# A hybrid SSD, gated and latent attention trunk: root of the first norm from logarithm and exponential, gates moved into the last scan step

## The chip, the cores and the metric

The kernel runs on one core of a Trainium2 chip. The metric is device time in microseconds (us), the median of the runs shown. Five engines work side by side, each through its own queue in order: TensorE (PE, matmuls; PEld are its weight loads), VectorE (DVE), ScalarE (ACT), GpSimd (POOL), and SyncE (SP), which here issues most of the transfers.

## The reference, cut to what matters

A trunk of two layers over 512 tokens of width 1024, in float32. The change lies in the first layer, of which this is the part that matters:

```python
h = rms_norm(x, mix_norm_even[j])              # x * rsqrt(mean(x*x) + 1e-6) * w
proj = h @ w_in
z, xbc, dt_raw, q, k, v, g, gk_low = jnp.split(proj, _offsets(IN_SIZES), axis=-1)
# scan mixer: 16 heads in 2 groups, chunks of 128 tokens
dt = jax.nn.softplus(dt_raw + dt_bias)
a_cum = jnp.cumsum(dt * -jnp.exp(a_log), axis=2)
y_ssd = rms_norm_per_group(scan(silu(conv(xbc)), dt, a_cum) * silu(z))
# gated mixer: 4 heads
gk = jax.nn.log_sigmoid(gk_low @ gk_w2 + gk_b) / 16
gcum = jnp.cumsum(gk.reshape(bsz, nc, Q, H, DK), axis=2)   # chunks of 64 tokens
q_dec = q * exp(gcum);  k_inv = k * exp(-gcum)
x = x + jnp.concatenate([y_ssd, y_gla], axis=-1) @ w_out
```

A dense SwiGLU layer, latent attention with 16 heads and a second dense layer follow; the change doesn't touch them.

## The kernel before

Everything is held transposed, 128 features on the partitions and 512 tokens in the row. Each dense product is exact to float32 by parts: every operand is split into a rounded half (`hi`) and a rest (`lo`), and `mm3` (L149) adds three products. `dense` (L154) runs it over 8 blocks of 128 features, so one output tile costs 24 matmuls. A weight tile of 512 KB goes through three steps (L130 to L147): a transfer into one of two raw buffers (`wraw`), a cast on ACT into one of three `whi` buffers, and a subtraction on DVE into one of three `wlo` buffers. Three PSUM banks (`acc`) take the dense products; a bank comes free when its product has been read. Four more banks serve small work: `st` and `a1` one each, `a2` two.

The order of the instructions on each engine is written by a planner before the run. It takes them in program order by readiness under its own cost estimates; `tc.high_priority(offset=n)` moves a block ahead by n instructions, and weights are moved ahead by 90 (`AHEAD`). Buffers are given out in that planned order too. The tiles of a pool that opens after another one closed wait until the closed pool's last reader of that memory is done.

First norm. The eight tiles of x are split (L207 to L214). The norm's factor R is not needed for the dense products, only where their results are read. ACT squares each tile into one of two `sq` buffers, DVE adds them up one after another (L218 to L231), and `rstd` (L173 to L197) sums over partitions with two matmuls into `st` and takes the root on DVE: ten instructions in a row, from a bit trick and two refinement steps. `tok_scalar` (L237) turns R into one number for each token. Behind it stand the product for the step widths and the gates' low rank, `dg` (L292), and the steps: softplus by a series of small instructions on DVE (L307 to L326), a cumulative sum by matmul (L334), and its copies (L336 to L343).

Scan mixer. Eight steps f, two heads each. `conv(i)` (L351) is a dense product, read with R into `xpad` (L358), a four tap convolution and a silu; `z_gate` (L390) a dense product and a silu; `core` (L396) the scan of the two heads, whose tile `mt` has two buffers (L407). After every fourth step `group_norm` (L460) normalises the four tiles of its group (`rstd`, then L464) and splits them into the parts `mxh` and `mxl` (L126, L127), which `out_round` (L267) multiplies by the output weights. In step 7 stand `out_round(0)` and `values(2)` ahead of `core(7)`. `values(h)` (L470) makes the values of one gated head: two weight tiles and 96 matmuls of 256 columns. `values(3)` stands behind `core(7)` and `group_norm(1)` (L505).

Gated mixer. Its pool `gp` opens when the scan's pool `sp` has closed. First come the gates: weights (L513 to L522), four products (L527), their absolute values and minima (L528, L529), Exp (L530), Ln (L531), a subtraction (L532) and four running sums on DVE (L534). `inner(h)` (L542) then makes q (read into `qd`, L558) and k, calls `out_round(1)` for head 0, and goes on to the scores (L594 to L596), the state and the outputs; `outer(h)` multiplies by the output gate.

Of the kernel before, what the change touches and what calls it, by code (L numbers as in the profile page):

```python
# [8 lines left out]
F32 = mybir.dt.float32  # L9
# [9 lines left out]
P = 128  # L19
# [6 lines left out]
AHEAD = 90  # L26
VALUES = (2, 3, 7)
# [19 lines left out]
def kernel(ctx: ExitStack, tc: tile.TileContext, A, yT, stop=99):  # L47
# [11 lines left out]
    def nm(s):  # L59
        cnt[0] += 1  # L60
        return f"{s}_{cnt[0]}"
# [30 lines left out]
    V.memset(warm, 0.0)  # L92
    S.activation(warm, warm, AF.Square)
# [7 lines left out]
    def col(name, i=0, lo=0, hi=P):  # L101
        j = PV[name] + i
        return pv[lo:hi, j:j + 1]
# [16 lines left out]


# [27 lines left out]
    def mm3(out, ah, al, bh, bl, first, last):  # L149
        E.matmul(out, ah, bh, start=first, stop=False)  # L150
        E.matmul(out, ah, bl, start=False, stop=False)  # L151
        E.matmul(out, al, bh, start=False, stop=last)  # L152

    def dense(ps, w, xs):  # L154

        n = len(xs)
        for k, (xh, xl) in enumerate(xs):
            mm3(ps, w[0][:, k, :], w[1][:, k, :], xh, xl, k == 0, k == n - 1)
# [39 lines left out]

    class Norm:
# [18 lines left out]
        def square(self, c, behind=None):  # L218
            x = X[c]
            sq = res.tile([P, T], F32, tag="sq", name=nm("sq"), bufs=2)  # L220
            i = S.activation(sq, x, AF.Square)
            if behind is not None:
                tc.add_manual_dep(i.ins, behind.ins.name,
                                  mybir.DependencyInfo(mybir.DependencyClass.NoSync,
                                                       mybir.DependencyReason.DATA),
                                  reason="squares once all parts are split")
# [35 lines left out]
    for c in range(KD):  # L262
        nrm.square(c, nrm.last)
    R = nrm.done()
# [21 lines left out]
    with tc.tile_pool(name="gkp", bufs=1) as gkp:  # L286
        rtok = tok_scalar(R)
# [15 lines left out]
        nc.sync.dma_start(alog, A["a_log"].partition_broadcast(P))  # L303

        ps = aux()
        for c in range(4):
            E.transpose(ps[:, 16 * c:16 * c + 16], dg[0:16, c * P:(c + 1) * P], ident[0:16, 0:16])  # L307
        dr = gkp.tile([P, 4, 16], F32, name="dr")
        V.tensor_tensor(dr, ps[:, :64].rearrange("p (c h) -> p c h", c=4),
                        dtb.unsqueeze(1).to_broadcast([P, 4, 16]), ALU.add)  # L310
        da = gkp.tile([P, 4, 16], F32, name="da")
        S.activation(da, dr, AF.Abs)
        S.activation(da, da, AF.Exp, scale=-1.0)
        db = gkp.tile([P, 4, 16], F32, name="db")
        V.tensor_scalar(db, da, 2.0, None, ALU.add)
        V.reciprocal(db, db)
        V.tensor_tensor(da, da, db, ALU.mult)
        V.tensor_tensor(db, da, da, ALU.mult)
        dp = gkp.tile([P, 4, 16], F32, name="dp")
        V.tensor_scalar(dp, db, 1.0 / 15, None, ALU.mult)  # L320
        for n in (13, 11, 9, 7, 5, 3):
            V.scalar_tensor_tensor(dp, dp, 1.0 / n, db, ALU.add, ALU.mult)  # L322
        V.scalar_tensor_tensor(dp, dp, 1.0, da, ALU.add, ALU.mult)
        V.tensor_scalar(dr, dr, 0.0, None, ALU.max)
        dt = gkp.tile([P, 4, 16], F32, name="dt")
        V.scalar_tensor_tensor(dt, dp, 2.0, dr, ALU.mult, ALU.add)  # L326
        av = gkp.tile([P, 16], F32, name="av")
        S.activation(av, alog, AF.Exp)
        at = gkp.tile([P, 4, 16], F32, name="at")
        V.scalar_tensor_tensor(at, dt, -1.0, av.unsqueeze(1).to_broadcast([P, 4, 16]),  # L330
                               ALU.mult, ALU.mult)
        ps = aux()
        for c in range(4):
            E.matmul(ps[:16, c * P:(c + 1) * P], at[:, c, :], tri, start=True, stop=True)  # L334
        acf = gkp.tile([16, T], F32, name="acf")
        V.tensor_copy(acf, ps[:16])  # L336
        acd = dpool.tile([16, T], F32, name="acd")
        nc.sync.dma_start(acd, acf)
        ps = aux()
        for c in range(4):  # L340
            E.transpose(ps[:, 16 * c:16 * c + 16], acf[:, c * P:(c + 1) * P], ident[0:16, 0:16])
        act = gkp.tile([P, 4, 16], F32, name="act")
        V.tensor_copy(act, ps[:, :64].rearrange("p (c h) -> p c h", c=4))  # L343


        with tc.tile_pool(name="ssd", bufs=2) as sp:
# [3 lines left out]

            def conv(i, tag, bufs, bank=acc):  # L351
# [3 lines left out]
                dense(ps, w, xp)  # L355
# [127 lines left out]

            rounds = []
            for f in range(8):
# [19 lines left out]
            values(3)  # L505


        with tc.tile_pool(name="gla", bufs=2) as gp:
            rmask = gp.tile([P, T], F32, name="rmask", bufs=1)
            G.memset(rmask, 1.0)  # L510
            G.memset(rmask.rearrange("p (c j) -> p c j", c=8)[:, :, 0:1], 0.0)
            gw = gp.tile([80, T], F32R, name="gw", bufs=1)
            G.memset(gw.bitcast(I32), 0)  # L513
            w2 = res.tile([P, T], F32, tag="sq", name="w2", bufs=2)
            wt = res.tile([P, T], F32R, tag="sq", name="wt", bufs=2)
            for j in (0, 32, 64):
                nc.scalar.dma_start(w2[j:j + 16, :], A["gk_w2"])
            S.copy(wt[0:16, :], w2[0:16, :])
            V.tensor_tensor(gw[0:16, :], w2[0:16, :], wt[0:16, :].bitcast(F32), ALU.subtract)
            for j in (32, 64):  # L520
                S.copy(gw[j:j + 16, :], w2[j:j + 16, :])

            ga = gp.tile([P, 4, T], F32, name="ga", bufs=1)
            gm = gp.tile([P, 4, T], F32, name="gm", bufs=1)
            for h in range(4):
                ps = aux()
                E.matmul(ps, gw[:, h * P:(h + 1) * P], gx, start=True, stop=True)  # L527
                S.activation(ga[:, h, :], ps, AF.Abs, bias=col("gk_b", h))  # L528
                V.tensor_scalar(gm[:, h, :], ps, col("gk_b", h), 0.0, ALU.add, ALU.min)  # L529
            S.activation(ga, ga, AF.Exp, scale=-1.0)  # L530
            S.activation(ga, ga, AF.Ln, bias=1.0)  # L531
            V.tensor_tensor(gm, gm, ga, ALU.subtract)  # L532
            for h in range(4):
                V.tensor_tensor_scan(gm[:, h, :], rmask, gm[:, h, :], 0.0, ALU.mult, ALU.add)  # L534
# [122 lines left out]
            p01 += outer(1, o1)  # L657
            o3 = inner(3)
# [399 lines left out]
```

## Time and profile before

| what | us |
|---|---|
| median of 3 runs | 1372.63 |
| lowest, highest | 1371.01, 1373.25 |
| the profiled execution's own time | 1371.09 |
| its span | 1368.9 |

The span is the time from the first to the last instruction; 2.2 us of the profiled execution's time lie around it. Matmuls overlap: the profile gives one of 512 columns a duration of 0.39 us, but in a full stream one starts every 0.227 us. A row of the timeline gives start, duration, engine, line, operation, output and inputs, shapes, a count, and in brackets the engine's idle time before it and what ended that.

### The profile page before, as it was taken

To read this page: it belongs to the slowest core of one execution; us is meant where nothing else is said; L and a number is where in the kernel's file an instruction comes from. 1 tells how busy PE (TensorE), PEld (TensorE's weight loads), DVE (VectorE), ACT (ScalarE), POOL (GpSimd) and SP (SyncE) were. 2 spreads that over 40 slices of the span, in tenths; PEclk is the share of its full clock that TensorE was granted. 3 is DMA by queue.
4 is the path that set the end of the run, shared out by engine and by line. 5 is a ranking of instruction groups with operands and counts; after the bars stand their busy time and mean duration, and the time that the engine had idled before them with its cause. 6 is when DMAs were issued, how large, how long until landed. Compare 5 with 4: busy or idle time off the path is not lost.

```text
span 1368.9 us, 16667 instructions
## 1 busy us (share of the span) xinstructions
PE 1344.9 (98%) x6506; PEld 1088.7 (80%) x6506; DVE 815.5 (60%) x1369; ACT 562.8 (41%) x941; POOL 7.8 (1%) x35
## 2 busy tenths in 40 slices
PE   8999999999999999999999999999999999999998
PEld 5788889788888888888888887666588888888887
DVE  7987976788867444444333469776594444443221
ACT  5584633544344322332232348775653322322121
POOL 0000000000000000000000000000000000000000
PEclk9999999999999999999999999999999999999999
DMA  5342232222233333223333321111033223323331
GB/s 177 109 141 91 77 95 78 78 77 62 79 93 105 93 94 106 92 92 99 90 100 100 101 68 56 39 47 62 1 98 103 93 93 102 98 93 108 111 103 63
DMA packets 36781, 122.22 MB, mean 89 GB/s; under 512 B 4768, under 2 KB 5792, under 8 KB 36704
## 3 DMA queue, kind: packets, MB, share of 16 engines
q1 hardware_dynamic: 35888, 120.72, 28.1%
q8 instruction: 51, 0.84, 0.2%
q10 hardware_dynamic: 816, 0.46, 0.1%
q14 instruction: 26, 0.21, 0.0%
HBM read 119.03 MB, written 2.13 MB: 89 GB/s over the span
## 4 chain that ended last, share of the span: by engine, by line
PE 90%; DVE 5%; ACT 3%; issue 1%; DMA 1%; SPq 0%; ACTq 0%
PE acc L150 27%; PE acc L151 27%; PE acc L152 27%; PE sco L911 2%; PE ptr L925 1%; PE po L934 1%; DVE wlo L145 1%; PE a L447 1%; PE a L625 0%; PE a L433 0%; PE a L614 0%; PE a L451 0%; ACT whi L144 0%; PE a L627 0%; DVE gm L534 0%
## 5 line engine op out<-in xcount | busy, mean ns | idle before, releaser
L150 PE MATMUL acc<-xh,whi 128*128 128x512 f32 x1144 | 449.1, 393 | 5.2 <-DVE dp L322 2.5
L144 ACT CAST whi<-wraw 128x1024 fp32r<-128x1024 f32 (+2 forms) x221 | 225.8, 1022 | 554.0 <-PE acc L151 436.9
L151 PE MATMUL acc<-xl,whi 128*128 128x512 f32 x1144 | 448.7, 392 | 0.0
L152 PE MATMUL acc<-xh,wlo 128*128 128x512 f32 x1144 | 448.7, 392 | 0.0
L145 DVE TENSOR_TENSOR wlo<-wraw,whi 128x1024 fp32r<-128x1024 f32 (+2 forms) x221 | 261.9, 1185 | 163.2 <-ACT whi L144 163.1
L150 PEld LDWEIGHTS acc<-xh,whi 128*128 128x128 f32 x1144 | 214.9, 188 | 51.2 <-ACT cvt L366 2.8
L152 PEld LDWEIGHTS acc<-xh,wlo 128*128 128x128 f32 x1144 | 215.1, 188 | 44.8 <-DVE wlo L145 0.6
L151 PEld LDWEIGHTS acc<-xl,whi 128*128 128x128 f32 x1144 | 215.1, 188 | 44.5 <-issue 1.4
L152 PE MATMUL acc<-fhh,wlo 128*128 128x512 f32 x288 | 112.0, 389 | 0.0
L150 PE MATMUL acc<-fhh,whi 128*128 128x512 f32 x288 | 112.0, 389 | 0.0
L151 PE MATMUL acc<-fhl,whi 128*128 128x512 f32 x288 | 112.0, 389 | 0.0
L683 DVE TENSOR_TENSOR fu<-acc,R 128x512 f32<-128x512 f32 x44 | 30.4, 691 | 136.2 <-PE acc L152 136.2
L680 DVE TENSOR_TENSOR fg<-acc,R 128x512 f32<-128x512 f32 x44 | 30.4, 691 | 89.0 <-PE acc L152 88.9
L152 PEld LDWEIGHTS acc<-fhh,wlo 128*128 128x128 f32 x288 | 54.1, 188 | 11.3
L151 PEld LDWEIGHTS acc<-fhl,whi 128*128 128x128 f32 x288 | 54.1, 188 | 11.3
L150 PEld LDWEIGHTS acc<-fhh,whi 128*128 128x128 f32 x288 | 54.1, 188 | 11.1
L151 PE MATMUL acc<-mxl,whi 128*128 128x512 f32 x128 | 49.9, 391 | 0.0
L150 PE MATMUL acc<-mxh,whi 128*128 128x512 f32 x128 | 49.8, 391 | 0.0
L152 PE MATMUL acc<-mxh,wlo 128*128 128x512 f32 x128 | 49.7, 390 | 0.0
L911 PE MATMUL sco<-kT,qT 96*128 96x128 f32 (+3 forms) x128 | 42.8, 445 | 1.5 <-DVE mx L914 1.3
L914 DVE CUSTOM_DVE_ANT_0 sc<-sco,am 128x128 f32<-128x128 f32 (+3 forms) x64 | 30.7, 487 | 13.6 <-PE sco L911 11.5
L916 ACT ACTIVATE sc<-sc,mx 128x128 f32<-128x128 f32 (+3 forms) x64 | 35.7, 561 | 7.3 <-DVE mx L914 6.8
(329 smaller groups left out, 1584.8 us busy)
## 6 DMA issues: line engine op xcount, KB each, us to landing
wraw<-in_w_gate_dram SPq DMA_DIRECT2D x44, 512.0 KB, 3.5
wraw<-in_w_up_dram SPq DMA_DIRECT2D x44, 512.0 KB, 3.5
wraw<-in_w_down_dram SPq DMA_DIRECT2D x32, 512.0 KB, 3.6
wraw<-in_w_out_dram SPq DMA_DIRECT2D x16, 512.0 KB, 3.6
wraw<-in_w_xbc_dram SPq DMA_DIRECT2D x12, 512.0 KB, 3.6
wraw<-in_w_down_dram SPq DMA_DIRECT2D x16, 384.0 KB, 3.1
wraw<-in_w_z_dram SPq DMA_DIRECT2D x8, 512.0 KB, 3.5
wraw<-in_w_v_dram SPq DMA_DIRECT2D x8, 512.0 KB, 3.5
```

The source lines that it names most:

```text
L144: S.copy(hi[:, :kc * m], r)
L145: V.tensor_tensor(lo[:, :kc * m], r, hi.bitcast(F32)[:, :kc * m], ALU.subtract)
L150: E.matmul(out, ah, bh, start=first, stop=False)
L151: E.matmul(out, ah, bl, start=False, stop=False)
L152: E.matmul(out, al, bh, start=False, stop=last)
L447: E.matmul(pd[64 * h:64 * h + 64, c * P:(c + 1) * P], xdt[:, c, h, :], mt[:, h, c, :], start=True, stop=True)
L680: V.tensor_tensor(g, pg, R, ALU.mult)
L683: V.tensor_tensor(u, pu, R, ALU.mult)
L911: E.matmul(ps[:, :n], qts[j][:, b * P:(b + 1) * P], kts[j][:, :n], start=True, stop=True)
L914: V.tensor_tensor_reduce(sc[:, :n], ps[:, :n], am[:, T - n:], -scale, 3e38, ALU.add, ALU.min, mx[:, j:j + 1])
L916: S.activation(sc[:, :n], sc[:, :n], AF.Exp, bias=mx[:, j:j + 1], scale=-1.0, accum_out=sm[:, j:j + 1])
L925: E.transpose(ps[:, kb * P:(kb + 1) * P], sc[:, kb * P:(kb + 1) * P], ident)
```

## The change

Four parts.

1. The first norm: its squares go into four buffers of a pool of their own, and `rstd_log` replaces `rstd` there. R is the exponential of minus half the logarithm (both on ACT), followed by one refinement step on DVE. The block is moved ahead by 400. The dummy activation at the start is a Ln instead of a Square.
2. The steps are moved behind the last matmul of the product of `conv(0)` and ahead by 150; `tok_scalar` moves to step 2, where `values(0)` first reads it.
3. The gates move from the start of the gated mixer into step 7, ahead of `out_round(0)`. Their temporaries take buffers of the scan (`cva`, `cvt`, and the two `mt` buffers), Exp and Ln run on halves, and eight running sums of 256 columns replace four of 512. `gm` and `rmask` lie in the outer pool.
4. `values(3)` moves from behind the last scan step to a place behind `outer(1)`, into a buffer of the pool `gp`.

```diff
 AHEAD = 90
+FIRST = 400
+STEPS = 150
 VALUES = (2, 3, 7)
...
-    V.memset(warm, 0.0)
-    S.activation(warm, warm, AF.Square)
+    V.memset(warm, 1.0)
+    S.activation(warm, warm, AF.Ln)
+    eps = const.tile([P, 1], F32, name="eps")
+    V.memset(eps, EPS)
...
+    def order(i, behind, reason):
+
+        tc.add_manual_dep(i.ins, behind.ins.name,
+                          mybir.DependencyInfo(mybir.DependencyClass.NoSync, mybir.DependencyReason.DATA),
+                          reason=reason)
...
-            mm3(ps, w[0][:, k, :], w[1][:, k, :], xh, xl, k == 0, k == n - 1)
+            last = mm3(ps, w[0][:, k, :], w[1][:, k, :], xh, xl, k == 0, k == n - 1)
+        return last
...
+    def rstd_log(ssq, n, pool, tag):
+
+        hi = const.tile([P, T], F32R, tag="rsa", name=nm("rsa"))
+        lo = const.tile([P, T], F32R, tag="rsb", name=nm("rsb"))
+        S.copy(hi, ssq)
+        V.tensor_tensor(lo, ssq, hi.bitcast(F32), ALU.subtract)
+        ps = aux()
+        E.matmul(ps, ones_r, hi, start=True, stop=False)
+        E.matmul(ps, ones_r, lo, start=False, stop=True)
+        R = pool.tile([P, T], F32, tag=tag, name=nm(tag), bufs=1)
+        S.activation(R, ps, AF.Ln, scale=1.0 / n, bias=eps)
+        S.activation(R, R, AF.Exp, scale=-0.5)
+        m, t = ssq, const.tile([P, T], F32, tag="rsa", name=nm("rst"))
+        V.tensor_scalar(m, ps, 1.0 / n, EPS, ALU.mult, ALU.add)
+        V.tensor_tensor(t, R, R, ALU.mult)
+        V.scalar_tensor_tensor(t, m, -0.5, t, ALU.mult, ALU.mult)
+        V.scalar_tensor_tensor(R, t, 1.5, R, ALU.add, ALU.mult)
+        return R
...
-        def square(self, c, behind=None):
+        def square(self, c, behind=None, pool=res, bufs=2):
             x = X[c]
-            sq = res.tile([P, T], F32, tag="sq", name=nm("sq"), bufs=2)
+            sq = pool.tile([P, T], F32, tag="sq", name=nm("sq"), bufs=bufs)
             i = S.activation(sq, x, AF.Square)
             if behind is not None:
-                tc.add_manual_dep(i.ins, behind.ins.name,
...
-    for c in range(KD):
-        nrm.square(c, nrm.last)
-    R = nrm.done()
+    with tc.tile_pool(name="sq0", bufs=4) as sq0:
+        for c in range(KD):
+            nrm.square(c, nrm.last, sq0, 4)
+        with tc.high_priority(offset=FIRST):
+            R = rstd_log(nrm.ssq, D, res, "R")
...
-        rtok = tok_scalar(R)
...
+        def steps(behind):
+
+
+            ps = aux()
+            for c in range(4):
+                i = E.transpose(ps[:, 16 * c:16 * c + 16], dg[0:16, c * P:(c + 1) * P], ident[0:16, 0:16])
+                order(i, behind, "steps behind the product that runs until they are ready")
+            dr = gkp.tile([P, 4, 16], F32, name="dr")
+            V.tensor_tensor(dr, ps[:, :64].rearrange("p (c h) -> p c h", c=4),
...
+            acf = res.tile([P, T], F32, tag="sq", name="acf", bufs=2)[:16]
...
+            return dt, act, acd
...
-                dense(ps, w, xp)
+                mm[i] = dense(ps, w, xp)
...
-            def values(h):
+            def values(h, pool=gkp):
...
-                v = gkp.tile([P, 4, 256], F32, name=f"v{h}")
+                v = pool.tile([P, 4, 256], F32, name=f"v{h}", bufs=1)
...
+            gm = gkp.tile([P, 4, T], F32, name="gm")
+
+            rmask = gkp.tile([P, T // 2], F32, name="rmask")
+            G.memset(rmask, 1.0)
+            G.memset(rmask.rearrange("p (c j) -> p c j", c=4)[:, :, 0:1], 0.0)
+
+            def gates():
+
+                gw = sp.tile([80, T], F32R, tag="cvt", name="gw")
+                G.memset(gw.bitcast(I32), 0)
+                w2 = sp.tile([P, T], F32, tag="cva", name="w2")
+                wt = sp.tile([P, T], F32R, tag="cvt", name="wt")
+                for j in (0, 32, 64):
+                    nc.scalar.dma_start(w2[j:j + 16, :], A["gk_w2"])
+                S.copy(wt[0:16, :], w2[0:16, :])
+                V.tensor_tensor(gw[0:16, :], w2[0:16, :], wt[0:16, :].bitcast(F32), ALU.subtract)
+                for j in (32, 64):
+                    S.copy(gw[j:j + 16, :], w2[j:j + 16, :])
+                gas = [sp.tile([P, 2, T], F32, tag="mt", name=nm("ga")) for _ in range(2)]
+                for h in range(4):
+                    ps = aux()
+                    E.matmul(ps, gw[:, h * P:(h + 1) * P], gx, start=True, stop=True)
+                    S.activation(gas[h // 2][:, h % 2, :], ps, AF.Abs, bias=col("gk_b", h))
+                    V.tensor_scalar(gm[:, h, :], ps, col("gk_b", h), 0.0, ALU.add, ALU.min)
+                for ga in gas:
+                    S.activation(ga, ga, AF.Exp, scale=-1.0)
+                for ga in gas:
+                    S.activation(ga, ga, AF.Ln, bias=1.0)
+                for j, ga in enumerate(gas):
+                    V.tensor_tensor(gm[:, 2 * j:2 * j + 2], gm[:, 2 * j:2 * j + 2], ga, ALU.subtract)
+                for h in range(4):
+                    for t0 in (0, T // 2):
+                        gj = gm[:, h, t0:t0 + T // 2]
+                        V.tensor_tensor_scan(gj, rmask, gj, 0.0, ALU.mult, ALU.add)
...
+                if f == 0:
+                    with tc.high_priority(offset=STEPS):
+                        dt, act, acd = steps(mm[0])
                 zg = z_gate(f)
                 if f == R0F:
+                    gates()
                     out_round(0, rounds[0])
+                if f == VALUES[0]:
+                    rtok = tok_scalar(R)
                 if f in VALUES:
                     values(VALUES.index(f))
...
-            values(3)
...
-            rmask = gp.tile([P, T], F32, name="rmask", bufs=1)
-            G.memset(rmask, 1.0)
-            G.memset(rmask.rearrange("p (c j) -> p c j", c=8)[:, :, 0:1], 0.0)
-            gw = gp.tile([80, T], F32R, name="gw", bufs=1)
-            G.memset(gw.bitcast(I32), 0)
-            w2 = res.tile([P, T], F32, tag="sq", name="w2", bufs=2)
...
             p01 += outer(1, o1)
+            values(3, gp)
             o3 = inner(3)
```

## Rows read from the trace of the kernel before

**Rows 1.** Busy time of two engines over the span, from the page: engine, us and share, count of instructions.

```profile
PE 1344.9 (98%) x6506; PEld 1088.7 (80%) x6506; DVE 815.5 (60%) x1369; ACT 562.8 (41%) x941; POOL 7.8 (1%) x35
```

**Rows 2.** Waits of PE over the whole span: who waited, for whom, us in total, times, longest.

```profile
PE acc L150 <- DVE dp L322: 2.5, 1, 2.5
...
PE a L594 <- DVE ki L575: 1.9, 1, 1.9
...
PE st L181 <- ACT rsa L178: 1.0, 1, 1.0
...
PE a L152 <- DVE wlo L145: 0.5, 1, 0.5
...
PE a L150 <- ACT whi L144: 0.4, 1, 0.4
```

**Rows 3.** Timeline of PE at two of these waits.

```profile
43.33 0.39 PE L151 MATMUL acc<-xl,whi 128*128 128x512 f32 x1
43.56 0.39 PE L152 MATMUL acc<-xh,wlo 128*128 128x512 f32 x1
46.40 0.47 PE L150 MATMUL acc<-xh,whi 128*128 128x512 f32 x1 [2.46 <-DVE dp L322]
...
263.39 0.39 PE L152 MATMUL acc<-xh,wlo 128*128 128x512 f32 x1
265.66 0.27 PE L594 MATMUL a<-qd,ki 128*64 128x64 f32 x1 [1.88 <-DVE ki L575]
```

**Rows 4.** Busy time by stretch: the stretch, then for each engine us and count, then PE's granted clock as a share of 2.4 GHz, DMA share, GB/s.

```profile
44.00:47.00 3.00, 0.60 (x3) 0.54 (x4) 3.00 (x9) 2.08 (x3) 0.10 (x1) 1.00 0.00 0
...
263.00:265.00 2.00, 0.78 (x4) 0.32 (x2) 2.00 (x4) 0.96 (x1) 0.00 (x0) 1.00 0.01 4
...
267.00:269.00 2.00, 2.00 (x7) 1.56 (x6) 2.00 (x4) 0.84 (x3) 0.00 (x0) 0.58 0.00 0
269.00:270.30 1.30, 1.30 (x6) 0.55 (x6) 0.81 (x2) 0.31 (x1) 0.00 (x0) 0.50 0.00 0
```

**Rows 5.** Timeline of ACT and of DVE in the first norm: first squares, the rounded sum of squares, first and last instruction of the root, and the reading of the first `acc` bank.

```profile
10.47 1.14 ACT L221 ACTIVATE sq<-x 128x512 f32<-128x512 f32 x2
...
24.38 0.62 ACT L178 CAST rsa<-sq 128x512 fp32r<-128x512 f32 x1 [0.76 <-DVE sq L230]
...
26.34 0.69 DVE L186 TENSOR_SCALAR sq<-st 128x512 f32<-128x512 f32 x1 [0.61 <-PE st L182]
...
34.44 0.68 DVE L196 SCALAR_TENSOR_TENSOR R<-rst,R 128x512 f32<-128x512 f32 x1
...
45.58 0.68 DVE L358 TENSOR_TENSOR xpad<-acc,R 128x512 f32<-128x512 f32 x1
```

**Rows 6.** Timeline of ACT and DVE in the gates: an activation that reads PSUM, two table loads, an Exp of 512 columns, the subtraction and the running sums.

```profile
250.22 0.69 ACT L528 ACTIVATE ga<-st,pv 128x512 f32<-128x512 f32 x1 [1.87 <-PE st L527]
...
253.81 1.28 ACT L531 ACT_TABLE_LOAD   x1
...
258.55 1.28 ACT L549 ACT_TABLE_LOAD   x1
...
261.24 0.62 ACT L556 ACTIVATE e<-gm 128x512 f32<-128x512 f32 x1
...
257.05 2.29 DVE L532 TENSOR_TENSOR gm<-gm,ga 128x2048 f32<-128x2048 f32 x1 [1.38 <-ACT ga L531]
...
259.86 4.56 DVE L534 TENSOR_TENSOR_SCAN gm<-rmask,gm 128x512 f32<-128x512 f32 x4
```

**Rows 7.** Timeline from the last scan step to the second output round: on PE the first transposes of `core(7)`, the first matmul of q of head 0 and the first of `out_round(1)`; on DVE the splits of the normalised group and the first reading of q; on POOL the first write into the pool `gp`.

```profile
213.15 0.60 PE L422 MATMUL a<-ident,xs 128*128 128x128 f32 x4
...
228.81 0.40 PE L150 MATMUL acc<-xh,whi 128*128 128x512 f32 x1
...
239.71 0.39 PE L150 MATMUL acc<-mxh,whi 128*128 128x512 f32 x1
...
236.04 1.89 DVE L127 TENSOR_TENSOR mxl<-y,mxh 128x512 fp32r<-128x512 f32 x3
...
239.64 0.68 DVE L127 TENSOR_TENSOR mxl<-y,mxh 128x512 fp32r<-128x512 f32 x1
240.36 0.69 DVE L558 SCALAR_TENSOR_TENSOR qd<-acc,R 128x512 f32<-128x512 f32 x1
...
240.52 0.53 POOL L510 MEMSET rmask<- 128x512 f32 x1 [83.59 <-DVE mxl L127]
```

**Rows 8.** Timeline of PE: first and last of the 96 matmuls of `values(2)`.

```profile
201.63 0.28 PE L150 MATMUL acc<-whi,xh 128*128 128x256 f32 x1
...
213.03 0.28 PE L152 MATMUL acc<-whi,xl 128*128 128x256 f32 x1
```

**Rows 9.** Weights and the other engines around the last scan step: DVE's weight rests from 213 to 240.4 us as a group (count, busy us and mean ns, idle time before), a cast on ACT with what it waited for, and busy time by stretch as in rows 4.

```profile
L145 DVE TENSOR_TENSOR wlo<-wraw,whi 128x1024 fp32r<-128x1024 f32 x5 | 6.1, 1221 | 9.1 <-ACT whi L144 9.1
...
234.29 1.05 ACT L144 CAST whi<-wraw 128x1024 fp32r<-128x1024 f32 x1 [0.35 <-PE acc L151]
...
195.00:205.00 10.00, 10.00 (x59) 8.83 (x59) 4.51 (x5) 2.40 (x3) 0.00 (x0) 1.00 0.28 101
205.00:213.00 8.00, 8.00 (x69) 8.00 (x68) 0.01 (x1) 2.18 (x4) 0.00 (x0) 1.00 0.18 61
```

More of the change, by code (lines that the diff above doesn't have):

```diff
@@ L151, in mm3 @@
         E.matmul(out, ah, bl, start=False, stop=False)
-        E.matmul(out, al, bh, start=False, stop=last)
+        return E.matmul(out, al, bh, start=False, stop=last)
     def dense(ps, w, xs):
@@ L216, in add @@
                 self.square(c)
-        def square(self, c, behind=None):
+        def square(self, c, behind=None, pool=res, bufs=2):
             x = X[c]
-            sq = res.tile([P, T], F32, tag="sq", name=nm("sq"), bufs=2)
+            sq = pool.tile([P, T], F32, tag="sq", name=nm("sq"), bufs=bufs)
             i = S.activation(sq, x, AF.Square)
             if behind is not None:
-                tc.add_manual_dep(i.ins, behind.ins.name,
-                                  mybir.DependencyInfo(mybir.DependencyClass.NoSync,
-                                                       mybir.DependencyReason.DATA),
-                                  reason="squares once all parts are split")
+                order(i, behind, "squares once all parts are split")
             if self.ssq is None:
@@ L303 @@
         nc.sync.dma_start(alog, A["a_log"].partition_broadcast(P))
[L305 to L342, printed above, removed]
@@ L343 @@
-        V.tensor_copy(act, ps[:, :64].rearrange("p (c h) -> p c h", c=4))
+        def steps(behind):
[5 more added lines that the diff above has]
+            V.tensor_tensor(dr, ps[:, :64].rearrange("p (c h) -> p c h", c=4),
+                            dtb.unsqueeze(1).to_broadcast([P, 4, 16]), ALU.add)
+            da = gkp.tile([P, 4, 16], F32, name="da")
+            S.activation(da, dr, AF.Abs)
+            S.activation(da, da, AF.Exp, scale=-1.0)
+            db = gkp.tile([P, 4, 16], F32, name="db")
+            V.tensor_scalar(db, da, 2.0, None, ALU.add)
+            V.reciprocal(db, db)
+            V.tensor_tensor(da, da, db, ALU.mult)
+            V.tensor_tensor(db, da, da, ALU.mult)
+            dp = gkp.tile([P, 4, 16], F32, name="dp")
+            V.tensor_scalar(dp, db, 1.0 / 15, None, ALU.mult)
+            for n in (13, 11, 9, 7, 5, 3):
+                V.scalar_tensor_tensor(dp, dp, 1.0 / n, db, ALU.add, ALU.mult)
+            V.scalar_tensor_tensor(dp, dp, 1.0, da, ALU.add, ALU.mult)
+            V.tensor_scalar(dr, dr, 0.0, None, ALU.max)
+            dt = gkp.tile([P, 4, 16], F32, name="dt")
+            V.scalar_tensor_tensor(dt, dp, 2.0, dr, ALU.mult, ALU.add)
+            av = gkp.tile([P, 16], F32, name="av")
+            S.activation(av, alog, AF.Exp)
+            at = gkp.tile([P, 4, 16], F32, name="at")
+            V.scalar_tensor_tensor(at, dt, -1.0, av.unsqueeze(1).to_broadcast([P, 4, 16]),
+                                   ALU.mult, ALU.mult)
+            ps = aux()
+            for c in range(4):
+                E.matmul(ps[:16, c * P:(c + 1) * P], at[:, c, :], tri, start=True, stop=True)
+            acf = res.tile([P, T], F32, tag="sq", name="acf", bufs=2)[:16]
+            V.tensor_copy(acf, ps[:16])
+            acd = dpool.tile([16, T], F32, name="acd")
+            nc.sync.dma_start(acd, acf)
+            ps = aux()
+            for c in range(4):
+                E.transpose(ps[:, 16 * c:16 * c + 16], acf[:, c * P:(c + 1) * P], ident[0:16, 0:16])
+            act = gkp.tile([P, 4, 16], F32, name="act")
+            V.tensor_copy(act, ps[:, :64].rearrange("p (c h) -> p c h", c=4))
+            return dt, act, acd
@@ L349 @@
             V.tensor_scalar(cw, pv[:, j:j + 60], 0.5, None, ALU.mult)
+            mm = {}
             def conv(i, tag, bufs, bank=acc):
```

20 lines of the change are left out of this document (1 added, 19 removed).

## The prediction

> **What bounds the kernel now.** I read the page's busy times first: PE is busy for 1344.9 of 1368.9 us [rows 1]. The change adds and removes no matmul (`rstd_log` keeps the two sums, gates, steps and `values(3)` keep theirs), so it can only move PE's 24 us of idle time and its clock. Second came PE's waits [rows 2]. In the stretch that the change touches they are: 2.5 us for a dense product of the scan, 1.9 us for the first scores of the gated mixer, 1.0 us for the sum of squares, and 0.5 and 0.4 us for the first weights. Third, the timeline at the two long ones [rows 3]. In a full stream a matmul starts 0.23 us behind the last (43.33, 43.56). The gap to 46.40 is 2.84 us, so 2.6 us are lost; the gap from 263.39 to 265.66 is 2.27 us, 2.0 us lost. Fourth, the granted clock [rows 4]: behind the second gap it reads 0.58 for 2.0 us and 0.50 for 1.3 us (0.50 is 1.2 GHz, 1.00 is 2.4 GHz), which costs 2.0 x 0.42 + 1.3 x 0.50 = 1.5 us. Behind the first gap it stayed at 1.00.
>
> **The change part by part**, against the profiled execution's 1371.09 us.
>
> *First norm.* Squares and sums run from 10.47 to 24.38 us, the root from 26.34 to 35.12 us [rows 5]: 8.8 us. With four buffers ACT no longer waits for each sum. What is left in that stretch is 8 squares, 7 sums and four weight splits; DVE needs 7 x 0.69 (the row of L186 has the same shape) + 4 x 1.22 [rows 9] = 9.7 us, so the sum is ready some 3.5 us earlier. The new root is Ln from PSUM 0.69 (nearest row the activation L528), a table load 1.28, Exp 0.62 [rows 6], and three DVE instructions of 0.69 on the path (the fourth, `m`, runs beside Ln): 4.7 us, or 6.0 with a second load ahead of Ln. That there is a load between Ln and Exp I take from the trace: Ln at L531 has one and the next Exp, L549, has another [rows 6]. R comes 3.5 + 8.8 - 4.7 = 7.6 us earlier, at about 27.5.
>
> What that is worth: the stall at 46.40 is a product that wants an `acc` bank. The wait names a small softplus instruction, but the bank comes free with the reading at 45.58 to 46.26 [rows 5], which stood in a queue behind R. Moved by 7 us, it ends at about 39, and PE wants it at 43.8. The stall goes: -2.6 us (bounds -2.6 and 0, were the reading to stay late). The 1.0 us wait for the rounded sum I leave as it is, since PE will again reach that matmul a little ahead of the engines (bounds -1.2 and +1.5). The two weight waits of 0.5 and 0.4 us stay too: without the steps ahead of them the first weights gain places against the squares, which may help, or make ACT wait for a transfer (bounds -0.9 and +1.2).
>
> *Steps and `tok_scalar`.* The same instructions in another place. They leave the full DVE stretch around 45 us (3.00 of 3.00 busy [rows 4]) and nothing waits for `tok_scalar` before step 2. Cost nothing; cover is the dense product of `z_gate(0)`. Were the planner to put their matmuls where DVE's chain of small instructions isn't done, PE would wait up to 1.5 us.
>
> *Gates.* In the gated mixer they end with 2.29 us of subtraction and 4.56 us of sums [rows 6], the last of which hold up qd and ki, for which PE waits at 265.66. Done in step 7 they are long ready: -2.0 us for the gap and -1.5 us for the slow clock behind it, -3.5 us. In step 7 there is room: from 195 to 213 us DVE is busy for 4.5 of 18 us and ACT for 4.6 [rows 9]. POOL's memsets and the three transfers on ACT's queue go with them. Those wait there for a `cva` buffer, with weight casts queued behind: 0 to 1 us, taken at nothing, because PE has dense work with casts two tiles ahead.
>
> *`values(3)`.* At its new place behind `outer(1)` its two transfers on SP, two splits and four readings stand where PE has no wait [rows 2]. At its old place it was cover. From the first transposes of `core(7)` at 213.15 to the first matmul of `out_round(1)` at 239.71 [rows 7] PE is busy for 26.6 us, and what it does there is `values(3)`, q and k of head 0, and some 4 us of scan. `values(3)` is as long as `values(2)`: 201.63 to 213.03 and one start more [rows 8], 11.5 us. Without it PE is through with k at 26.6 - 11.5 = 15.1 us behind the first transposes.
>
> `out_round(1)` needs the normalised group. That chain is one instruction behind another on DVE and ACT: its splits end at 239.64 + 0.68 = 240.32 [rows 7], 27.2 us behind the transposes. The first three of four blocks of `out_round(1)` can run ahead of the last split (9 matmuls, 2.0 us), so PE could have started at 25.1 us. Five weight rests of 1.22 us stand in DVE's queue in that stretch [rows 9]; with the two weights of `values(3)` gone and later ones moving up I count four, 1.2 us less: 23.9 us. PE is idle for 23.9 - 15.1 = 8.8 us. Bounds: all five rests out of the chain, 25.1 - 6.1 - 15.1 = 3.9 us; the chain as it was, 10.0 us.
>
> Can anything else run there? q of head 1 is next in program order but stands behind the four weights of `out_round(1)`. Casts wait for PE to give back one of three buffers (the one at 234.29 for PE [rows 9]), and these will be held by `out_round(1)`. The rest of head 0 writes into the pool `gp`, and its first writes, qd at 240.36 and the memset at 240.52, came only when the last reader of `sp`, the split at 239.64, was through [rows 7]. So nothing.
>
> Behind so long a gap I expect the slow clock once more: +1.5 us, as behind the gap at 263.39; bounds 0, as behind the one at 43.56, and 3.0, two such stretches. The Trainium skill, page "TensorE: Matmul & The Clock Gate", section "Part 1: The HAM clock gate (the 'warmup' mystery)", says that "the default state is throttled, and activity releases the throttle". By that rule the slow stretch is certain, and the sum has the 1.5 us; by the row at 44 us it would have nothing. The trace agrees at one of its two gaps and not at the other.
>
> Sum: -2.6 - 3.5 + 8.8 + 1.5 = +4.2 us, 1375.3 us for an execution like the profiled one. The runs' median lies 1.5 us above that execution, so 1372.63 + 4.2 = 1376.8 us.
>
> **Rivals.**
>
> *The gap finds cover* (faster). The planner gives PE other work between k and `out_round(1)`: `core(7)` ahead of `values(2)`, or a weight of head 1 ahead of the output weights. For it: q and k of head 0 moved up in just this way before. Against it: program order held in every place that I read, and the three buffers. Then only the gains stay: 1372.63 - 6.1 = 1366.5 us. It decides from the point at which idle time and slow clock together fall below 6.1 us.
>
> *Gates and `core(7)` get in each other's way* (slower still). The gates' halves take both `mt` buffers, which `core(7)` needs too. If `core(7)` gets one first, two gates wait until its products are done, and their minima, half the subtraction and half the sums, 2 x 0.75 + 1.1 + 2.3 = 4.9 us of DVE (0.75 taken as the activation's 0.69 and a little), fall into the chain of the group norm. The gap grows by as much: 1376.8 + 4.9 = 1381.7 us. Against it: DVE is nearly idle before 213 us.
>
> *The first norm doesn't come early* (the change doesn't do what it says). An early Exp of the steps would put its table in place of Ln's, so that two loads, 2.6 us, stand in the chain, and ACT's queue could hold Ln behind casts. R would have to lose more than 4 of its 7.6 us before the stall at 46.40 comes back; then 1376.8 + 2.6 = 1379.4 us.
>
> **How the numbers follow.** Forecast 0.52, cover found 0.26, gates in the way 0.12, no early norm 0.10. The forecast's own range, with its idle time between 3.9 and 10.0 us, the clock between 0 and 3.0 and the first norm's bounds not all on one side, is 1372.0 to 1381.0 us. The range to 8 in 10 reaches down to the covered gap, 1366.0, and up to 1381.5. Within 0.2% of the time before, 2.7 us, is about what a measurement of this kernel can tell from no change. The forecast falls below that line in some 3 of 10 of its cases (0.16), and a half covered gap takes 0.02 from the first rival: same 0.18, faster 0.26 - 0.02 = 0.24, slower 0.36 + 0.12 + 0.10 = 0.58.
>
> **What would show it.** In the changed profile: the wait at about 44 to 46 us for a dense product is gone and R's last instruction ends before 31 us; a table load stands between Ln and Exp; no wait for `ki` at the first scores; and a new longest wait of PE, 6 to 10 us, on the first matmul of `out_round(1)` for `mxl` or `mxh`, with a granted clock near 0.5 behind it. Were PE's waits of the first 300 us to add up to less than now, I would be wrong about the cover, and the time would fall.

## The result and the profile after

The changed kernel takes 1378.02 us (median of five runs, 1377.8 to 1380.1), the kernel before 1373.25 us (1371.01 to 1373.93): a ratio of 1.0045, with an interval from 1.0031 to 1.0059. It is slower by 4 to 8 us; 4.2 us were predicted. The profiled execution takes 1377.99 us with a span of 1375.8 us, 6.9 us longer than the span before.

The waits of PE, in the same view and columns as [rows 2]:

```profile
PE acc L160 <- ACT mxh L136: 7.9, 1, 7.9
...
PE a L412 <- DVE cT L402: 1.3, 1, 1.3
...
PE a L467 <- DVE xde L462: 0.7, 1, 0.7
```

The waits for `dp`, `ki` and `rsa` of [rows 2] are gone. In their place stand a new longest wait in front of `out_round(1)` and a new one of 1.3 us in the first scan step. The timeline of PE there, against [rows 3] and [rows 7]: the first transposes of `core(7)`, the first products of `out_round(1)`, its last one and the first scores.

```profile
212.26 0.60 PE L456 MATMUL a<-ident,xs 128*128 128x128 f32 x4
...
236.02 0.79 PE L160 MATMUL acc<-mxh,whi 128*128 128x512 f32 x1 [7.89 <-ACT mxh L136]
237.30 0.80 PE L161 MATMUL acc<-mxl,whi 128*128 128x512 f32 x1 [0.48 <-DVE mxl L137]
...
261.32 0.39 PE L162 MATMUL acc<-mxh,wlo 128*128 128x512 f32 x1
261.64 0.27 PE L642 MATMUL a<-qd,ki 128*64 128x64 f32 x1
```

The scores follow `out_round(1)` without a wait; before they waited 1.88 us. `out_round(1)` itself, 96 products, takes 25.3 us from its first start to its last; before it took 23.0 us (239.71 to 262.71) with small work in between. The windows, in the columns of [rows 4], say why:

```profile
228.00:236.00 8.00, 0.14 (x1) 0.00 (x0) 7.76 (x12) 1.65 (x2) 0.00 (x0) 0.79 0.21 67
236.00:238.00 2.00, 1.49 (x3) 0.89 (x4) 2.00 (x4) 1.24 (x2) 0.00 (x0) 0.50 0.00 0
238.00:240.00 2.00, 2.00 (x6) 1.54 (x5) 1.32 (x3) 0.62 (x1) 0.00 (x0) 0.50 0.00 0
240.00:242.00 2.00, 2.00 (x6) 1.58 (x5) 1.97 (x4) 1.36 (x4) 0.99 (x2) 0.50 0.00 0
242.00:244.00 2.00, 2.00 (x8) 1.60 (x8) 2.00 (x5) 1.04 (x2) 0.00 (x0) 0.79 0.00 0
244.00:246.00 2.00, 2.00 (x11) 1.64 (x10) 1.12 (x2) 0.80 (x1) 0.00 (x0) 1.00 0.00 0
```

For 8 us PE does nothing while DVE is busy almost throughout; then it runs for more than 6 us at 0.50, 1.2 GHz, with six matmuls in a row of the table that holds eleven at 1.00.

The timeline of ACT and DVE in the first norm answers to [rows 5]: the rounded sum, the table loads ahead of Ln and ahead of Exp, the last instruction of R, and the reading of the first `acc` bank.

```profile
19.99 0.62 ACT L214 CAST rsa<-sq 128x512 fp32r<-128x512 f32 x1 [0.26 <-DVE sq L257]
...
21.61 1.28 ACT L220 ACT_TABLE_LOAD   x1
22.91 0.69 ACT L220 ACTIVATE R<-st,eps 128x512 f32<-128x512 f32 x1
23.61 1.28 ACT L221 ACT_TABLE_LOAD   x1
...
27.03 0.69 DVE L226 SCALAR_TENSOR_TENSOR R<-rst,R 128x512 f32<-128x512 f32 x1
...
36.34 0.63 DVE L392 TENSOR_TENSOR xpad<-acc,R 128x512 f32<-128x512 f32 x1
```

R is ready at 27.7 instead of 35.1 us, and the first bank is read 9.2 us earlier.

### The profile page after: what moved, and what is told of

It is laid out like the page before. It is cut to its first block, busy times and chain, and to the rows that moved or that the text cites. A ratio compares the mean times of both kernels' runs of the same rounds, so it can differ in the third digit from the quotient of the medians.

```text
span 1375.8 us, 16690 instructions
## 1 busy us (share of the span) xinstructions
PE 1347.7 (98%) x6506; PEld 1089.3 (79%) x6506; DVE 814.3 (59%) x1369; ACT 571.5 (42%) x950; POOL 7.8 (1%) x35
## 4 chain that ended last, share of the span: by engine, by line
PE 91%; DVE 5%; ACT 2%; issue 1%; DMA 0%; SPq 0%; DVEq 0%; ACTq 0%
PE acc L161 27%; PE acc L160 27%; PE acc L162 27%; PE sco L960 2%; PE ptr L974 1%; PE po L983 1%; DVE wlo L155 1%; PE a L481 1%; PE a L673 1%; PE a L467 0%; PE a L662 0%; PE a L485 0%; DMA x<-in_xT_dram 0%; ACT whi L154 0%; PE a L675 0%
## 5 line engine op out<-in xcount | busy, mean ns | idle before, releaser
L963 DVE CUSTOM_DVE_ANT_0 sc<-sco,am 128x128 f32<-128x128 f32 (+3 forms) x64 | 30.7, 488 | 13.6 <-PE sco L960 11.5
```

The costliest lines, as they stand in the source:

```text
L963: V.tensor_tensor_reduce(sc[:, :n], ps[:, :n], am[:, T - n:], -scale, 3e38, ALU.add, ALU.min, mx[:, j:j + 1])
```

## The experiments

Ratios are to the kernel before, run on the same chip. The median of before was 1373.69 us for the first four and 1373.06 us for the last three.

**Parts 1 and 2 alone.** The changed kernel with the gates and `values(3)` where they were before:

```diff
                 if f == R0F:
-                    gates()
                     out_round(0, rounds[0])
...
+            values(3)
...
         with tc.tile_pool(name="gla", bufs=2) as gp:
+            ga = gp.tile([P, 4, T], F32, name="ga", bufs=1)
+            gm = gp.tile([P, 4, T], F32, name="gm", bufs=1)
...
-            values(3, gp)
```

> The first two parts alone: squares in four buffers, root from logarithm and exponential, steps behind the product of conv(0); gates and values(3) stand where they stood before. Cover theory (the loss of the changed kernel is PE's gap ahead of out_round(1), because values(3) no longer covers the group norm): no gap, and the front is worth what the changed trace shows until core(7), 213.15 - 212.26 + 0.95 for the four gate products done earlier = 1.8 us: 1.8 us below before. Rival (the gates in step 7 hold up core(7) and the group norm, by two mt buffers and four table loads): the same here. If the first norm were the cause of the loss, this kernel would be above before.

Measured: 1369.46 us, ratio 0.9973 (0.9960 to 0.9986), 1.9 to 5.5 us faster, where 1.8 was expected. In its trace the stages from `values(2)` to `out_round(1)` start 2.5 us earlier than before (199.15 against 201.63 for the first matmul of `values(2)`), and `out_round(2)` 4.1 us earlier (356.71 against 360.81). The wait for `ki` is still there, but in this execution the clock behind it didn't fall, as a timeline and the windows of this run show:

```profile
263.13 0.27 PE L633 MATMUL a<-qd,ki 128*64 128x64 f32 x1 [1.81 <-DVE ki L614]
```

```profile
262.00:264.00 2.00, 0.87 (x7) 0.71 (x8) 2.00 (x5) 1.03 (x2) 0.00 (x0) 1.00 0.00 0
264.00:266.00 2.00, 2.00 (x10) 1.66 (x9) 2.00 (x5) 0.78 (x2) 0.00 (x0) 1.00 0.00 0
```

The profiled execution is the fastest of the eight and has a mean granted clock of 1.000; the others have 0.996 to 0.999. So the first half of the change is a gain by itself, in the trace of the size of the term predicted for it (2.6), and the loss lies in the second half.

**Only `values(3)` moved.** The kernel before with part 4 alone:

```diff
-            values(3)
...
             p01 += outer(1, o1)
+            values(3, gp)
```

> The kernel before with values(3) moved behind outer(1), nothing else. Cover theory: PE waits some 9 us for mxh or mxl at the first matmul of out_round(1), the clock falls to half for some 6 us behind it (3.4 us), and the wait of 1.9 us for ki stays: 11 to 13 us above before. Rival: without the gates in step 7 the chain of the group norm has nothing in its way, the gap is below 3 us and the time at most 4 us above before.

Measured: 1385.6 us, ratio 1.0079 (1.0061 to 1.0097), by the medians 11.9 us slower. The gap is the same as in the changed kernel, to 0.02 us, with the gates still in their old place:

```profile
237.82 0.80 PE L150 MATMUL acc<-mxh,whi 128*128 128x512 f32 x1 [7.87 <-ACT mxh L126]
```

The gap thus comes without the gates in step 7. `values(3)` was the cover, that is, TensorE work that ran while the chain on the other engines was under way, and taking it away costs 8.4 to 13.3 us; gap and slow clock were put at 10.3.

**Idle products in the gap.** The changed kernel with 34 products into a PSUM bank of their own that nobody reads, behind k of head 0. They add work and leave nothing out:

```diff
                 if after_dense is not None:
+                    with tc.tile_pool(name="pdum", bufs=1, space=PSUM) as pdum:
+                        ps = pdum.tile([P, T], F32, name="dum")
+                        for j in range(NDUM):
+                            i = E.matmul(ps, ones_r, xp[0][0], start=True, stop=True)
+                            order(i, kl, "idle products behind k")
                     after_dense()
```

> The changed kernel with 34 products into a spare bank behind k of head 0 (their result is read by nothing), which keep PE busy for 34 x 0.227 = 7.7 us where it was idle for 7.9. If the slow clock behind the gap is a price of its own: granted clock 1.00 through 228 to 248 us and 3.4 us below the changed kernel, so some 3 us above before. If the clock costs nothing, because something else is late behind the gap: the time of the changed kernel.

Measured: 1377.08 us (1376.52 to 1378.58), ratio 1.0027 (1.0017 to 1.0037), and a span 0.8 us under that of the changed kernel. The clock stays at full speed, as the windows show, but new waits come up within `out_round(1)`:

```profile
236.00:238.00 2.00, 1.23 (x5) 0.53 (x4) 2.00 (x4) 1.52 (x3) 0.00 (x0) 1.00 0.00 0
238.00:240.00 2.00, 1.73 (x8) 1.07 (x6) 1.42 (x3) 0.54 (x1) 0.00 (x0) 1.00 0.00 0
240.00:242.00 2.00, 1.64 (x5) 0.86 (x6) 1.86 (x3) 1.24 (x5) 0.99 (x2) 1.00 0.00 0
```

```profile
237.61 0.49 PE L162 MATMUL acc<-mxl,whi 128*128 128x512 f32 x1 [0.77 <-DVE mxl L138]
240.13 0.49 PE L161 MATMUL acc<-mxh,whi 128*128 128x512 f32 x1 [0.40 <-ACT mxh L137]
240.85 0.50 PE L162 MATMUL acc<-mxl,whi 128*128 128x512 f32 x1 [0.23 <-DVE mxl L138]
```

`out_round(1)` takes 24.2 us (236.34 to 260.54) instead of 25.3. With a clock at full speed PE only comes sooner to parts that aren't split yet. Of 3.3 us that the slow clock takes by the timeline (25.3 - 0.5 of wait, against 21.5 for the same 96 products without a wait, in the run with late second gates below), only 1.1 us are the clock's own price; the rest would have been lost to waiting for the last splits anyway. By the medians the idle products bring some 1 us, by the ratios 2.5, whose intervals overlap; the traces carry the smaller figure.

**Half of the gates moved, `values(3)` back.** With the whole of `gm` in the outer pool `values(3)` no longer fits in memory beside the scan. So the gates of heads 0 and 1 stay in step 7, those of heads 2 and 3 go back to the start of the gated mixer:

```diff
-            gm = gkp.tile([P, 4, T], F32, name="gm")
+            gm = gkp.tile([P, 2, T], F32, name="gm")
...
-            def gates():
+            def gates(h0, gw, w2, wt, ga, dst):
...
-                    gates()
+                    gates(0, sp.tile([80, T], F32R, tag="cvt", name="gw"),
...
+            values(3)
...
         with tc.tile_pool(name="gla", bufs=2) as gp:
+            gm2 = gp.tile([P, 2, T], F32, name="gm2", bufs=1)
+            gates(2, gp.tile([80, T], F32R, name="gw", bufs=1),
...
-            values(3, gp)
```

> The first two parts, the gates of heads 0 and 1 in step 7 and those of heads 2 and 3 at the start of the gated mixer, and values(3) back behind the last scan step (half the gates leave the memory that it needs). Cover theory: no wait of PE over 1 us from 50 to 830 us; 1.8 us from the front and 3.5 us from the wait for ki with its slow clock: 5 us below before. Rival: two gates in step 7 still take an mt buffer and their table loads, the group norm is late and PE waits 4 us or more for mxh: not below before.

Measured: 1368.38 us, ratio 0.9958 (0.9941 to 0.9974). There is no wait for `mxh` and none for `ki`; against the expectation one wait of PE of more than 1 us is new in the gated mixer:

```profile
255.63 0.50 PE L160 MATMUL acc<-mxh,whi 128*128 128x512 f32 x1 [1.72 <-DVE x L304]
```

It wants a bank of `out_round(1)` that is read late, since DVE is at the running sums of heads 2 and 3:

```profile
252.23 2.43 DVE L545 TENSOR_TENSOR_SCAN gm<-rmask,gm 128x256 f32<-128x256 f32 x4
...
254.89 1.28 DVE L304 TENSOR_TENSOR x<-x,acc 128x512 f32<-128x512 f32 x2
```

**The second half of the gates later.** The same, with the gates of heads 2 and 3 directly ahead of `inner(2)`, the first reader:

```diff
         with tc.tile_pool(name="gla", bufs=2) as gp:
             gm2 = gp.tile([P, 2, T], F32, name="gm2", bufs=1)
-            gates(2, gp.tile([80, T], F32R, name="gw", bufs=1),
...
             p01 = outer(0, o0)
+            gates(2, gp.tile([80, T], F32R, name="gw", bufs=1),
...
             o2 = inner(2)
```

> Parts 1 and 2, the gates of heads 0 and 1 in step 7, values(3) back behind the last scan step (as in the run with half the gates moved), but the gates of heads 2 and 3 stand directly ahead of inner(2) instead of at the start of the gated mixer. Theory: the 1.7 us wait at 255.6 us in front of a product of out_round(1), whose bank was read late because DVE was at the second half of the gates, goes, and no other comes, because ahead of inner(2) DVE has spare time: 1368.4 - 1.7 = 1366.7 us, a ratio to before of 0.994 to 0.996. Rival: the same 7 us of DVE work stand in the way at the new place too, before the reads of outer(0) or the q and k of head 2, and the wait comes back there: 1368.4 us or a little more.

Measured: 1365.65 us (1365.59 to 1367.22), ratio 0.9948 (0.9931 to 0.9965), 4.8 to 9.5 us faster than before and the fastest of all. The wait of 1.72 us is gone, and the span, 1363.9 us, is 2.5 us under the previous run's (0.9 of them because its first product starts earlier, at 5.22 instead of 6.11 us). A wait for `ki` of 1.0 us has come in at 323.76 us, in a later head, so the rival's mechanism exists too, at a smaller price.

**`values(2)` as cover.** The changed kernel with `values(2)` taken out of step 7 and put where `values(3)` used to be:

```diff
-                if f in VALUES:
+                if f in VALUES[:2]:
                     values(VALUES.index(f))
...
                     rounds.append(group_norm(g, ys, ssq))
+            values(2)
```

> The changed kernel with values(2) taken out of step 7 and put behind the last scan step; values(3) stays behind outer(1). Theory A, work on TensorE between the first transposes of core(7) and out_round(1) is all that is missing: 11.5 us of values(2) now stand there, the 7.9 + 0.5 us of wait in front of out_round(1) and the slow clock behind it (2.5 to 3.4 us) go, and no other wait of over 1 us comes, so 1378.0 - 8.4 - 2.5 = 1367.1 us, perhaps down to 1366.2. Theory B, the cover would not do with the gates where they are: core(7) is now reached 11 us earlier, at about 201 us, but its tile mt was ready only at 213 us in the changed kernel, behind the gates' activations, table loads and running sums. Then a new wait of 3 to 6 us stands in front of the products of core(7) for mt, the group norm is ready no earlier than 234 to 236 us, a gap of some 2 to 5 us is left in front of out_round(1), the two together are again about 8 us, and the time is 1375 to 1378 us. I hold B for the likelier, 6 to 4.

Measured: 1374.41 us, ratio 1.0009 (1.0000 to 1.0018), just under what I held for the likelier, and far from 1367.1. Both halves of that expectation show: a wait in `core(7)` and what is left in front of `out_round(1)`.

```profile
211.34 0.91 PE L467 MATMUL a<-xde,btok 128*128 128x128 f32 x6 [3.08 <-DVE xde L462]
...
230.81 0.50 PE L160 MATMUL acc<-mxh,whi 128*128 128x512 f32 x1 [0.27 <-ACT mxh L136]
232.08 0.49 PE L161 MATMUL acc<-mxl,whi 128*128 128x512 f32 x1 [0.77 <-DVE mxl L137]
233.35 0.58 PE L161 MATMUL acc<-mxl,whi 128*128 128x512 f32 x1 [0.31 <-DVE mxl L137]
```

The timeline of DVE shows what `core(7)` waits for. I had named `mt`; it was `xde`, in DVE's queue behind the gates' last running sums and the two halves of `mt`:

```profile
207.12 2.43 DVE L551 TENSOR_TENSOR_SCAN gm<-rmask,gm 128x256 f32<-128x256 f32 x4
209.46 1.27 DVE L448 TENSOR_TENSOR mt<-mt,cb 128x512 f32<-128x512 f32 x2
210.65 0.55 DVE L462 TENSOR_TENSOR xde<-xdt,te 128x384 f32<-128x384 f32 x1
```

The windows around the two places:

```profile
208.00:210.00 2.00, 0.27 (x3) 0.06 (x1) 2.00 (x4) 1.95 (x4) 0.00 (x0) 1.00 0.00 0
210.00:212.00 2.00, 0.66 (x6) 0.69 (x6) 2.00 (x4) 0.00 (x0) 0.00 (x0) 1.00 0.00 0
212.00:214.00 2.00, 2.00 (x25) 1.71 (x24) 1.75 (x6) 0.27 (x1) 0.00 (x0) 1.00 0.36 68
...
234.00:236.00 2.00, 2.00 (x6) 1.51 (x6) 2.00 (x3) 1.36 (x4) 0.99 (x2) 0.50 0.00 0
```

From this product of `core(7)` to the first of `out_round(1)` it is 19.5 us, as in the changed kernel (216.56 to 236.02), and 19.4 with only `values(3)` moved (218.39 to 237.82). So in these three kernels the chain behind `core(7)` has one length, and what makes `core(7)` start later moves all of it.

**All gates in step 3.** As the run before, but with the gates ahead of `values(1)`, far from the group norm:

```diff
                 if f == R0F:
-                    gates()
                     out_round(0, rounds[0])
...
+                if f == VALUES[1]:
+                    gates()
                 if f in VALUES[:2]:
```

> As the run with values(2) behind the last scan step, but with all gates in step 3, ahead of values(1), where no group norm follows closely behind. Theory B (the gates' hold on mt is what keeps core(7) late) says: mt of core(7) is ready early, no wait of over 1 us in core(7) and none in front of out_round(1), ratio to before 0.994 to 0.997, 1366 to 1369 us. If theory A holds, this run and the one with the gates left in step 7 come out within 1.5 us of each other. Rival: the gates in step 3 hold up the scan step there in the same way (core(3) waits for mt and the first group norm behind it comes late), which would show as a new wait of 3 us or more around the first out_round and 1370 us or more.

Measured: 1380.14 us, ratio 1.0051 (1.0036 to 1.0066): the rival. In front of `out_round(1)` the gap is gone altogether (it starts at 243.48, directly behind k at 243.25), but from the first transposes of `core(3)` to the first product of `out_round(0)` it is 84.1 us (111.34 to 195.39), where the changed kernel takes 68.6 us (108.67 to 177.22) for the same matmuls. The timeline of PE and the windows show where:

```profile
120.26 1.62 PE L467 MATMUL a<-xde,btok 128*128 128x128 f32 x6 [2.83 <-DVE xde L462]
123.63 0.80 PE L162 MATMUL acc<-xh,wlo 128*128 128x512 f32 x1 [0.90 <-DVE wlo L155]
...
163.32 0.50 PE L162 MATMUL acc<-xh,wlo 128*128 128x512 f32 x1 [3.40 <-DVE wlo L155]
```

```profile
112.00:120.00 8.00, 5.43 (x24) 4.13 (x22) 6.39 (x9) 7.94 (x14) 0.00 (x0) 1.00 0.00 1
120.00:125.00 5.00, 3.84 (x11) 2.61 (x11) 4.81 (x9) 4.97 (x8) 0.00 (x0) 0.51 0.38 127
125.00:130.00 5.00, 5.00 (x23) 3.39 (x23) 2.71 (x7) 2.96 (x11) 0.00 (x0) 0.50 0.42 163
...
160.00:164.00 4.00, 0.68 (x2) 0.39 (x3) 4.00 (x7) 0.00 (x0) 0.00 (x0) 1.00 0.00 0
```

While the gates' activations and table loads fill ACT (7.94 of 8 us), `core(3)` and the weight casts stand behind them; PE waits, and the clock falls to 0.50 for 10 us. A second stretch, which the changed kernel doesn't have either, lies at 160 to 164 us: DVE is busy throughout with instructions of the scan and of the first group norm, a weight's rest stands behind them, and PE does 0.68 us. That this one is a consequence of the first is argued, not shown. The gates need a place where DVE and ACT have slack, and of the two places tried step 7 with its dense work has more of it [rows 9].

## Why the prediction was right, and where it wasn't

The forecast case happened: the moved `values(3)` was cover. The whole ledger along PE, after minus before:

| point | before | after | shift |
|---|---|---|---|
| first transposes of `core(7)` | 213.15 | 212.26 | -0.9 |
| last matmul of k, head 0 | 239.49 | 227.75 | -11.7 |
| last matmul of `out_round(1)` | 262.71 | 261.32 | -1.4 |
| first matmul of `out_round(2)` | 360.81 | 368.49 | +7.7 |
| first matmul of `out_round(3)` | 394.23 | 401.15 | +6.9 |

**First norm: right.** The stall went, R was ready at 27.7 (predicted 27.5), and the trace has the predicted table load between Ln and Exp, and one more ahead of Ln. The time of R is in part luck: the rounded sum came 4.4 us earlier (24.38 against 19.99), where 3.5 was predicted, and the load ahead of Ln, not in the predicted sum, took the difference back. That load is the mechanism of the third rival (the Exp of `a_log` at 18.05 had put its own table in place); it was too short to bring the stall back. Alone the two parts bring 2.5 us along PE (predicted 2.6). In the changed kernel it is 1.8: -0.9 at `core(7)`, with some 0.9 us of the gates' four products already done there. The third product of the first weight tile, behind which the stream runs on, begins 0.64 us later in that trace than before (14.49 against 13.85), with the first two parts alone only 0.10 us later, inside the bounds that I gave to the weight waits; and the 1.0 us wait for `rsa`, which I had left as it is, went, while one of 1.3 us for `cT` came, so the two cancel.

**Gates: right, but not free.** No wait for `ki`, and one of 0.7 us in `core(7)` for `xde`. From the last matmul of `out_round(1)` to the first of `out_round(2)` it is 98.1 us before and 107.2 after, or 95.4 without the 11.8 us that `values(3)` takes there now: 2.7 us less. `out_round(1)` of before lasted 1.5 us longer than its own 96 products (23.0 against 21.5), for the gates' four products and what stood around them; 0.9 of that comes back in step 7. Together -3.2 us, predicted -3.5. The rival that gates and `core(7)` get in each other's way happened on a small scale: from the first transposes of `core(7)` to `xdt` on DVE it is 1.87 us (212.26 to 214.13), in the run with only `values(3)` moved 0.98 us (214.90 to 215.88). In both DVE does a weight's rest ahead of `xdt`; in the changed kernel that rest stands behind the gates' last sum and the second half of `mt`:

```profile
211.83 0.67 DVE L551 TENSOR_TENSOR_SCAN gm<-rmask,gm 128x256 f32<-128x256 f32 x1
212.41 0.67 DVE L448 TENSOR_TENSOR mt<-mt,cb 128x512 f32<-128x512 f32 x1
...
214.13 0.68 DVE L458 TENSOR_TENSOR xdt<-a,dt 128x512 f32<-128x512 f32 x1
```

In the run with only `values(3)` moved:

```profile
215.88 0.68 DVE L424 TENSOR_TENSOR xdt<-a,dt 128x512 f32<-128x512 f32 x1
```

The run with `values(2)` as cover shows the rival at 3.08 us: 11 us earlier, `xde` stands behind the gates.

**`values(3)`: the right mechanism, a term too small.** The step that failed is "with the two weights of `values(3)` gone and later ones moving up I count four, 1.2 us less: 23.9 us". The first product indeed came 23.76 us behind the transposes, and the gap of 7.9 us by itself is below the 8.8. But the last split ended 28.2 us behind them (240.49), not 26.0, so the nine products that can run ahead of it did not bridge the rest. Of these 2.2 us 0.9 are the gates' (above): with only `values(3)` moved, the last split ends 27.4 us behind the transposes (214.90 to 242.28). The count of the rests was right, their places were not. This is DVE in the changed kernel, from the reading of the scan's products to the last split:

```profile
222.80 1.23 DVE L155 TENSOR_TENSOR wlo<-wraw,whi 128x1024 fp32r<-128x1024 f32 x1 [0.83 <-ACT whi L154]
223.94 0.69 DVE L576 TENSOR_TENSOR ysq<-ysq,ysq 128x512 f32<-128x512 f32 x1
...
226.79 0.69 DVE L197 TENSOR_SCALAR ysq<-st 128x512 f32<-128x512 f32 x1 [0.78 <-PE st L193]
...
239.80 0.69 DVE L137 TENSOR_TENSOR mxl<-y,mxh 128x512 fp32r<-128x512 f32 x1 [0.68 <-ACT mxh L136]
```

A weight that moved up put its cast on ACT in front of the square (221.71; the square at 222.66, before at 221.96) and its rest in front of `ysq` at 222.80, and the next link shown, at 225.29 before, comes at 226.79; the 0.89 us by which PE reached `core(7)` earlier were lost on DVE at once (`xdt` at 214.13 in both kernels). With the clock at full speed, in the run with idle products, `out_round(1)` ends 32.5 us behind the end of k (228.29 to 260.77), against 21.8 for its 96 products: a loss of 10.7 us, where 8.8 was predicted and 10.0 was the bound.

**Slow clock: it came, and its price was nearly the predicted one by luck.** The sum had 1.5 us. The timeline shows 3.3 us, over my bound of 3.0, of which 1.1 us are left once what PE would have waited for is taken off. The Trainium skill's rule that I weighed ("TensorE: Matmul & The Clock Gate", section "Part 1: The HAM clock gate (the 'warmup' mystery)") is that the clock is throttled by default and activity releases it. The traces agree at both gaps of 7.9 us; behind the 3.08 us of the run with `values(2)` as cover and the 1.81 us of the first run the clock stayed at 1.00, so that there the slow stretch that I read out of the rule didn't come.

**The sum.** Terms of -2.6, -3.5, +8.8 and +1.5 were put at +4.2; along PE they measure -1.8, -3.2, +10.7 and +1.1, together +6.8. The spans differ by 6.9 us; smaller things (0.7 of wait for `xde`, `values(3)` 0.2 longer at its new place, 0.8 less in `out_round(2)`) cancel among themselves. The medians differ by 4.8 us, because the profiled execution of before lies 2.2 us under its median (1371.09 against 1373.25) and that of the changed kernel on its own. So it is luck that the forecast of 4.2 us came out so near: its terms along PE were 2.6 us too small. What the rival "the gap finds cover", put at -6.1 us, would have been worth is shown by the runs with `values(3)` back and half of the gates moved: -5.8 us (ratio 0.9958), and -7.1 us with the second gates placed late.

What stays open: why the clock falls behind one short gap and not behind another (below), and with it how much of the 3.7 us that parts 1 and 2 bring alone is the slow stretch behind the wait for `ki`, 1.5 us before, which that trace doesn't have and other executions of that kernel may have.

## What to carry to other kernels

Before moving a piece of dense work out of a dependent chain on other engines, count the chain from its start to the first product that needs it, and the TensorE work that stands beside it: `values(3)` looked like plain throughput and was 11.5 us of cover; taking it away alone cost 8.4 to 13.3 us, more than the change gained at its other places (5.0 us along PE). If memory forces the move, try to move only half of what displaced it. A chain's length depends on where the queue puts foreign instructions in it, and not only on how many there are: place the rests, don't only count them.

## What the runs showed of the hardware

- A gap's length alone does not decide what the clock does. In the profiled executions there was no fall behind a start-to-start gap of 2.84 us in the kernel before [rows 3, 4], behind idle times of 1.81 us (parts 1 and 2 alone) and 3.08 us (`values(2)` as cover), nor behind three of 1.4 us in all with the idle products. But it fell to 0.50 behind 1.88 us in the kernel before, behind 2.83 us with all gates in step 3, and behind three idle times of 1.35 us in all at 230 to 233 us in the run with `values(2)` as cover. Behind both gaps of 7.9 us it was at 0.50.
- The clock differs between executions of one kernel. Beside the first four experiments the kernel before ran 17 times, between 1370.86 us at a mean granted clock of 1.000 and 1377.11 us at 0.995. A trace shows only its own execution's clock.
- The slow clock is cheap where the engine would wait anyway: 3.3 us of slow running, 1.1 us of time.
- Ln and Exp never shared a table: each change between them brought a load of 1.28 us, in the first norm at 21.61 and 23.61 us, and in the gates, worked off in halves, four of them between 194 and 208 us. By the same count two would have done if both Exp had come before both Ln; no run shows it.
